# One block of a hybrid encoder in fp32: the gate/up products in another order, with banks of their own, their left factors made between the first products, and h stored by GpSimd

## The chip, the cores and the metric

The kernel runs on one core of a Trainium2 chip. The metric is the device time of one launch in microseconds; lower is better. The time before is 2817.62 us, the median of three runs (2817.23 to 2819.71).

## The reference

One layer of an encoder on a sequence of 512 tokens of width 2048, all in fp32: a mixing sub-layer (convolution, pooling, gated DeltaNet, Mamba-2), a cross-attention into 256 memory tokens, and a SwiGLU feed-forward with an inner width of 5632. Each sits between two norms and is added to the stream. What matters here is the third:

```python
def swiglu_ffn(h, w_gu, w_down):
    gate, up = jnp.split(h @ w_gu, 2, axis=-1)
    return (jax.nn.silu(gate) * up) @ w_down
...
x = x + rmsnorm(swiglu_ffn(rmsnorm(x, g[FFN_PRE]), ffn_w_gu[l], ffn_w_down[l]), g[FFN_POST])
```

## The kernel before

An fp32 product is made of three TensorE passes: each operand is split into a high part (a cast on ScalarE, L976) and a low part (source minus high part on VectorE, L977), and `mul3` (L168 to L171) adds high times high, high times low and low times high into one PSUM bank. The two large feed-forward products are worked by a seven-product scheme of 2x2 blocks in the manner of Strassen and Winograd: the activations give the left factors L1 to L7, the weights the right factors, and products M1 to M7 (numbered so in the code) are added into a few PSUM banks. On page and rows, L2h or B5l are left factors (number, high or low part) of the gate/up stage and of the down stage.

**Gate/up** (`gate_up`, L1019; `block`, L1073) runs over 44 blocks of 128 inner columns. A block loads four weight tiles of 0.5 MB (B11, B12, B21, B22), makes sums of them on VectorE (L1009 to L1016), splits each right factor into `whi` and `wlo`, and runs the products in `ORDER` (2, 1, 5, 6, 7, 3, 4), 24 matmuls each. M2 and M1 go into the two halves of one bank (`B` and `A` in `begin`, L1054); M2's half is copied out as `f_x` by ScalarE (L1067). M6, M7 and M4 are then added onto M1's half, where M6 is copied out as `f_y` (L1094) before M7 is added; M5 and M3 share a second bank `Cc`. The finished h tile (128 x 512) is stored to DRAM from SyncE's queue (L1108), which also loads all weights.

For the first five blocks M2 and M1 are made ahead of the others (`begin`), three of them while the second half of the normalised activations is still on its way. `left_parts` (L979) then makes L5, L6, L7, L3 and L4 for both 128-row halves (`sub`), all before block 0's five other products; their memory is opened at once, and the weight buffers `rp` and the work tiles `tp` are laid where the activations `stg` lay, so they wait for the last factor.

**Down** (`down`, L1124; `panel`, L1152) takes h back in five chunks of eight tiles, makes left factors B1 to B7 of each, and runs two panels per chunk, again seven products in `ORDER`, 24 matmuls of 512 columns each, with weights of 1 MB a tile (`rawB`, L1158). Results go to DRAM by GpSimd, which adds there.

Order on an engine is the order in which a list scheduler places the instructions; each engine's queue runs in that order, and SyncE's too: a store that waits holds up the loads behind it.

Of the kernel before, what the change touches and what calls it, by code (L numbers as in the profile page):

```python
# [7 lines left out]
F32 = mybir.dt.float32  # L8
# [7 lines left out]
P = 128  # L16
# [44 lines left out]

def build(tc, x, mem, norm_g, w_in, conv_a_w, pool_w, pool_scale, gdn_conv_w, gdn_A_log,
# [13 lines left out]
    es_act, es_ps, es_wp, es_stg, es_early = (ExitStack() for _ in range(5))  # L76
# [810 lines left out]
    def phase2(act):  # L887
        with ExitStack() as s0:
# [14 lines left out]
            stg = pool("stg", 8, "right", es_stg)  # L903
            yp = pool("yp2", stack=s0)
            pl2 = pool("adp2", stack=s0)
            xT = [[[stg.tile([P, 4, 256], F32, name="stg") for _ in range(2)] for _ in range(2)] for _ in range(2)]
# [66 lines left out]
    ORDER = (2, 1, 5, 6, 7, 3, 4)  # L973
# [5 lines left out]
    def left_parts(A11, A12, A21, A22, tmp, L, given=()):  # L979


        tt = nc.vector.tensor_tensor
        for m, a in ((2, A12), (1, A11)):
            if m not in given:
                split3(L[m], a)
                yield
        tt(tmp, A21, A22, op=ALU.subtract)
        split3(L[5], tmp)
        yield
        tt(tmp, tmp, A11, op=ALU.subtract)  # L990
        split3(L[6], tmp)
        yield
        tt(A21, A11, A21, op=ALU.subtract)
        split3(L[7], A21)
        yield
        tt(A12, A12, tmp, op=ALU.add)
        split3(L[3], A12)
        yield
        split3(L[4], A22)
        yield  # L1000

    def right_parts(B11, B12, B21, B22, new, begun=False):

        tt = nc.vector.tensor_tensor
        if not begun:
            yield B21
            yield B11
        p, t2 = new(), new()
        tt(p, B11, B12, op=ALU.add)  # L1009
        yield p  # L1010
        tt(t2, p, B22, op=ALU.add)
        yield t2
        tt(B12, B12, B22, op=ALU.add)
        yield B12
        yield B22
        tt(t2, t2, B21, op=ALU.add)  # L1016
        yield t2

    def gate_up(xT, L, begun):  # L1019

        with ExitStack() as s0:
            lp = pool("lp", 2, stack=s0, reuse_waits="tile")
            for m in ORDER[2:]:
                L[m] = [(lp.tile([P, 4, 256], F32R, name=f"L{m}h"), lp.tile([P, 4, 256], F32R, name=f"L{m}l"))
                        for _ in range(2)]
            with ExitStack() as s1:
# [4 lines left out]
                for _ in ORDER[2:]:  # L1031
                    for g in parts:
                        next(g)
# [293 lines left out]
```

## Time and profile before

| | us |
|---|---|
| median of three runs | 2817.62 |
| the profiled execution | 2815.95 |
| its span in the profile | 2814.2 |
| TensorE busy in the span | 2721.0 |
| VectorE, ScalarE, GpSimd busy | 1868.8, 1220.6, 115.9 |
| gate/up stage, first product of block 0 to last of block 43 | about 1411 to 2350 |
| down stage, both panels of five chunks | about 2363 to 2740 |

Times in rows are from the span's start; the execution is 1.75 us longer than its span. PE is TensorE, PEld its weight loads, DVE VectorE, ACT ScalarE, POOL GpSimd, SP SyncE. Matmuls overlap, so a busy PE says little about its pace: pace is read from start to start. `[x <-Y]` after a row is the idle time of the engine before it and what ended it.

### The profile page before, as it was taken

The page shows a single profiled execution, that of the slowest core. Times are in us where ns is not written, and L with a number is a line of the kernel's source. Part 1 is how long each engine was busy: PE and PEld are TensorE (multiplying, and loading weights), DVE is VectorE, ACT ScalarE, POOL GpSimd, SP SyncE. Part 2 cuts the span into 40 slices and gives each one's busy share as a digit, 9 for nine tenths or more (in the row PEclk, how much of TensorE's full clock was granted, in tenths as well). Part 3 has the DMA queues.
Part 4 walks back from the last instruction along what each step waited for, and adds up shares of the span by engine and source line. Part 5 has one row for each costly group of instructions (what it writes and reads, how often), then busy time and mean ns, then how long its engine had stood idle before and what let it go on. Part 6 is the DMA issues. An engine that isn't in the chain of part 4 may idle for free. (4 is left out here: it accounts for less than half of the span.)

```text
span 2814.2 us, 39887 instructions
## 1 busy us (share of the span) xinstructions
PE 2721.0 (97%) x15890; PEld 2384.8 (85%) x15890; DVE 1868.8 (66%) x2693; ACT 1220.6 (43%) x1874; POOL 115.9 (4%) x175
## 2 busy tenths in 40 slices
PE   8999999999999999999869999999999997999997
PEld 6788788878788878888769999999999997888885
DVE  5736557455752273343788777777777778999976
ACT  5623433233552253433554444444444444556542
POOL 0000001100000010000000000000000000000002
PEclk9999999999999999999989999999999999999998
DMA  8633322335574277523644333333333335577656
GB/s 294 226 102 95 89 68 79 113 120 168 191 276 176 96 260 240 165 90 131 212 157 148 117 117 113 124 109 117 113 114 123 112 110 213 186 192 198 169 144 222
DMA packets 161589, 428.38 MB, mean 152 GB/s; under 512 B 18157, under 2 KB 29306, under 8 KB 150522
## 3 DMA queue, kind: packets, MB, share of 16 engines
q1 hardware_dynamic: 146490, 367.10, 39.3%
q0 software_dynamic: 14912, 58.73, 7.6%
q8 instruction: 124, 2.03, 0.3%
q14 instruction: 63, 0.52, 0.1%
HBM read 351.30 MB, written 74.47 MB: 151 GB/s over the span
## 5 line engine op out<-in xcount | busy, mean ns | idle before, releaser
L154 DVE SCALAR_TENSOR_TENSOR wlo<-raw,PA,whi 128x512 fp32r<-128x512 f32 x368 | 263.2, 747 | 297.9 <-ACT whi L153 297.7
L153 ACT ACTIVATE whi<-raw,PA 128x512 fp32r<-128x512 f32 x368 | 247.7, 718 | 398.0 <-PE mm L170 213.8
L169 PE MATMUL mm<-act,whi 128*128 128x512 f32 x832 | 330.4, 397 | 0.0
L171 PE MATMUL mm<-act,wlo 128*128 128x512 f32 x832 | 327.3, 393 | 0.0
L170 PE MATMUL mm<-act,whi 128*128 128x512 f32 x832 | 326.8, 393 | 0.0
L976 ACT CAST whi<-raw 128x1024 fp32r<-128x1024 f32 x176 | 184.8, 1050 | 308.8 <-PE mm L170 262.2
L169 PE MATMUL mm<-whi,act 128*128 128x512 f32 x640 | 252.2, 395 | 1.9 <-ACT act L150 1.9
L170 PE MATMUL mm<-wlo,act 128*128 128x512 f32 x640 | 251.2, 393 | 1.8 <-DVE wlo L154 1.8
L171 PE MATMUL mm<-whi,act 128*128 128x512 f32 x640 | 250.5, 392 | 0.2 <-DVE act L151 0.2
L977 DVE TENSOR_TENSOR wlo<-raw,whi 128x1024 fp32r<-128x1024 f32 x176 | 215.5, 1226 | 49.2 <-ACT whi L976 48.7
L151 DVE TENSOR_TENSOR wlo<-raw,whi 128x1024 fp32r<-128x1024 f32 x92 | 112.4, 1224 | 192.9 <-ACT whi L150 192.8
L976 ACT CAST whi<-sum 128x1024 fp32r<-128x1024 f32 x132 | 138.5, 1050 | 215.8 <-PE mm L170 213.8
L977 DVE TENSOR_TENSOR wlo<-sum,whi 128x1024 fp32r<-128x1024 f32 x132 | 161.3, 1223 | 74.9 <-ACT whi L976 74.9
L171 PEld LDWEIGHTS mm<-act,wlo 128*128 128x128 f32 x832 | 156.8, 188 | 32.1 <-issue 0.5
L169 PEld LDWEIGHTS mm<-act,whi 128*128 128x128 f32 x832 | 156.9, 189 | 31.0 <-issue 0.7
L170 PEld LDWEIGHTS mm<-act,whi 128*128 128x128 f32 x832 | 156.8, 188 | 30.9 <-issue 0.7
L150 ACT CAST whi<-raw 128x1024 fp32r<-128x1024 f32 x92 | 96.8, 1053 | 186.7 <-PE mm L171 139.1
L169 PEld LDWEIGHTS mm<-whi,act 128*128 128x128 f32 x640 | 120.8, 189 | 28.3 <-ACT act L150 3.7
L170 PEld LDWEIGHTS mm<-wlo,act 128*128 128x128 f32 x640 | 120.9, 189 | 26.9 <-DVE wlo L154 2.7
L171 PEld LDWEIGHTS mm<-whi,act 128*128 128x128 f32 x640 | 120.6, 188 | 25.3 <-DVE act L151 0.6
L171 PE MATMUL mm<-L2h,wlo 128*128 128x256 f32 x352 | 101.1, 288 | 17.6 <-DVE wlo L977 17.6
L976 ACT CAST whB<-rawB 128x1024 fp32r<-128x1024 f32 x80 | 84.0, 1053 | 53.8 <-PE mm L171 52.1
(541 smaller groups left out, 7268.6 us busy)
## 6 DMA issues: line engine op xcount, KB each, us to landing
raw<-in_w_gu_dram SPq DMA_DIRECT2D x186, 512.0 KB, 3.4
raw<-in_w_in_dram SPq DMA_DIRECT2D x88, 512.0 KB, 3.6
rawB<-in_w_down_dram SPq DMA_DIRECT2D x40, 1024.0 KB, 6.2
raw<-in_xa_wkv_dram SPq DMA_DIRECT2D x64, 512.0 KB, 4.6
raw<-in_w_out_dram SPq DMA_DIRECT2D x32, 512.0 KB, 3.7
raw<-in_xa_wo_dram SPq DMA_DIRECT2D x32, 512.0 KB, 6.0
raw<-in_xa_wq_dram SPq DMA_DIRECT2D x32, 512.0 KB, 3.8
raw<-vw_d SPq DMA_DIRECT2D x28, 512.0 KB, 4.2
```

The costliest lines, as they stand in the source:

```text
L150: nc.scalar.copy(hi, src)
L151: nc.vector.tensor_tensor(lo, src, hi.bitcast(F32), op=ALU.subtract)
L153: nc.scalar.activation(hi, src, AF.Copy, scale=scale)
L154: nc.vector.scalar_tensor_tensor(lo, src, scale, hi.bitcast(F32), op0=ALU.mult, op1=ALU.subtract)
L169: nc.tensor.matmul(o, ah, bh, start=start, stop=False, skip_group_check=reopen)
L170: nc.tensor.matmul(o, ah, bl, start=False, stop=False, skip_group_check=reopen)
L171: nc.tensor.matmul(o, al, bh, start=False, stop=stop, skip_group_check=reopen)
L976: nc.scalar.copy(hl[0], src)
L977: nc.vector.tensor_tensor(hl[1], src, hl[0].bitcast(F32), op=ALU.subtract)
```

## The change

The order of the products becomes 1, 2, 6, 5, 7, 3, 4 in both stages, with weight tiles loaded in the order in which this needs them. In gate/up, M1 has the half bank `A` for itself and M2 a bank of the `ps` pool; what is copied out as `f_x` is M1, and the gate is formed from M2's bank. Block 0 runs in the order 5, 6, 7, 4, 3, and one left factor is made ahead of each of its products, with the early products of blocks 3 and 4 in between; memory of the activations is given back in three steps. The tile for h is single, and GpSimd's queue stores it.

```diff
-    ORDER = (2, 1, 5, 6, 7, 3, 4)
+    ORDER = (1, 2, 6, 5, 7, 3, 4)
+    FIRST = (5, 6, 7, 4, 3)
...
+        def sums(m):
+            if m in have:
+                return
+            have.add(m)
+            if m == 5:
+                tt(tmp, A21, A22, op=ALU.subtract)
+            elif m == 6:
+                sums(5)
+                sums(7)
+                tt(A11, tmp, A11, op=ALU.subtract)
+            elif m == 7:
+                sums(5)
+                tt(A21, A11, A21, op=ALU.subtract)
+            elif m == 3:
+                sums(6)
+                tt(A12, A12, A11, op=ALU.add)
+        for m in order:
+            sums(m)
+            split3(L[m], {1: A11, 2: A12, 3: A12, 4: A22, 5: tmp, 6: A11, 7: A21}[m])
+            if m == 7:
+                sums(3)
+            yield m
...
+            rp = pool("rp", 3, stack=s0, reuse_waits="tile")
+            tp = pool("tp", 2, stack=s0, reuse_waits="tile")
+            first = block(0, L, rp, tp, begun[0], FIRST)
+
+            def step():
+                for g in parts:
+                    next(g)
+                next(first)
+            step()
+            step()
+            begun[3] = begin(3, L, tp)
+            step()
             es_stg.close()
+            factor("lp4", 4)
+            step()
+            begun[4] = begin(4, L, tp)
+            es_a22.close()
+            factor("lp3", 3)
+            step()
...
+        if begun:
+            A, g = begun
+        else:
+            A, B = half(mm, "mm"), half(ps, "ps")
+            X, g = tl("x"), tl("g", 3)
+            product(A, split_w(next(parts)), L, 1)
+            nc.scalar.copy(X, A)
+            product(B, split_w(next(parts)), L, 2)
+            gate(g, B, X)
+        Cc = half(ps, "ps")
...
-        h = tp.tile([P, T], F32, name="f_h")
+        h = tp.tile([P, T], F32, name="f_h", bufs=1)
...
-        nc.sync.dma_start(h_d[j], h)
+            if m != order[-1]:
+                yield
+        nc.gpsimd.dma_start(h_d[j], h)
...
-            if m == 2:
+            if m == 1:
                 X = new("eX")
-                copy(X, B)
-            elif m == 1:
+                copy(X, A)
+            elif m == 2:
                 for t in range(2):
-                    tt(X[:, t], A[t], X[:, t], op=ALU.add)
+                    tt(X[:, t], B[t], X[:, t], op=ALU.add)
```

The changed line numbers are larger by 8 to 49 (`mul3` is at L176 to L179, the split at L988 and L989).

**First place.** TensorE in a block of gate/up before: the first matmul of each run of one left factor, and those that wait (`ps` is the bank `Cc`).

```order
L169 MATMUL mm<-L2h,whi 128x256 [waits Activation_49]
L171 MATMUL mm<-L2h,wlo 128x256 [waits DVE_49]
...
L169 MATMUL ps<-L5h,whi 128x256 [waits Activation_49]
L171 MATMUL ps<-L5h,wlo 128x256 [waits DVE_49]
...
L169 MATMUL mm<-L1h,whi 128x256 [waits Activation_49]
...
L169 MATMUL mm<-L6h,whi 128x256 [waits DVE_49]
...
L169 MATMUL mm<-L7h,whi 128x256 [waits Activation_49]
```

And now:

```order
L177 MATMUL mm<-L1h,whi 128x256 [waits Activation_49]
L179 MATMUL mm<-L1h,wlo 128x256 [waits DVE_49]
...
L177 MATMUL ps<-L2h,whi 128x256 [waits Activation_49]
...
L177 MATMUL mm<-L6h,whi 128x256 [waits Activation_49]
...
L177 MATMUL ps<-L5h,whi 128x256
L179 MATMUL ps<-L5h,wlo 128x256 [waits DVE_49]
...
L177 MATMUL mm<-L7h,whi 128x256 [waits Activation_49]
```

Before, 11 matmuls of M5 stand between M2 and M1 and the other 13 behind M1, and M3 is cut in the same way around M7. Now each product stands whole, with one product of 24 matmuls between a product and the next one that is added to its bank.

**Second place.** VectorE where the left factors are made, before (`tmp` and `stg` are sums and activations, `wlo<-raw` a right factor's low part).

```order
L977 TENSOR_TENSOR L5l<-tmp_11498,L5h 128x1024 [waits Activation_49]
...
L977 TENSOR_TENSOR L7l<-stg,L7h 128x1024 [waits Activation_49]
L977 TENSOR_TENSOR L3l<-stg,L3h 128x1024 [waits Activation_49] x2
L977 TENSOR_TENSOR L4l<-stg,L4h 128x1024 x2
L977 TENSOR_TENSOR wlo<-raw,whi 128x1024 [waits DMAHW4_49]
L977 TENSOR_TENSOR wlo<-raw,whi 128x1024 [waits DMAHW5_49]
```

And now:

```order
L989 TENSOR_TENSOR L5l<-tmp,L5h 128x1024 [waits Activation_49]
L1027 TENSOR_TENSOR sum<-raw 128x1024 [waits DMAHW6_49,DMAHW4_49,DMASW2_49]
...
L1009 TENSOR_TENSOR stg<-stg 128x1024
L1105 TENSOR_TENSOR f_g<-mm,f_x 128x256 [waits PE_49]
L989 TENSOR_TENSOR wlo<-sum,whi 128x1024 [waits Activation_49]
...
L1030 TENSOR_TENSOR sum<-sum,raw 128x1024 [waits DMAHW7_49]
L989 TENSOR_TENSOR L6l<-stg,L6h 128x1024 [waits Activation_49]
```

The first right factor's low part stood behind all ten left factors' low parts; now M5's stands behind two of them, and M6's after three.

**Third place.** SyncE at the end of gate/up, before and now (`hq` is a quarter of a chunk of h).

```order
L1120 DMA hq<-h_d 128x4x256 [waits DMAHW6_49]
L1108 DMA h_d<-f_h 128x512 [waits DMAHW7_49,DVE_49]
L1158 DMA rawB<-in_w_down_dram 128x2048 [waits DMAHW0_49,PE_49]
L1158 DMA rawB<-in_w_down_dram 128x2048 [waits DMAHW1_49,PE_49]
L1158 DMA rawB<-in_w_down_dram 128x2048 [waits DMAHW2_49]
```

```order
L1168 DMA hq<-h_d 128x4x256 [waits DMAHW3_49]
L1208 DMA rawB<-in_w_down_dram 128x2048 [waits DMAHW4_49,PE_49]
L1208 DMA rawB<-in_w_down_dram 128x2048 [waits DMAHW5_49,PE_49]
L1208 DMA rawB<-in_w_down_dram 128x2048 [waits DMAHW6_49,PE_49]
L1208 DMA rawB<-in_w_down_dram 128x2048 [waits DMAHW7_49]
```

And ScalarE there, before and now:

```order
L976 CAST B7h<-hq 128x1024 [waits DVE_49,Activation_49]
L976 CAST B6h<-tmp 128x1024 [waits DVE_49]
L976 CAST B3h<-hq 128x1024 [waits DVE_49]
L976 CAST whB<-rawB 128x1024 [waits DMAHW2_49,DMASW3_49,DMASW1_49]
L976 CAST whB<-rawB 128x1024 [waits Activation_49]
```

```order
L988 CAST B7h<-hq 128x1024 [waits DVE_49,Activation_49]
L988 CAST whB<-rawB 128x1024 [waits DMAHW4_49]
L988 CAST whB<-rawB 128x1024 [waits DMASW4_49,DMASW5_49,DMASW3_49,DMASW6_49,DMASW2_49,DMASW7_49,DMASW1_49,DMASW0_49]
L988 CAST B6h<-hq 128x1024 [waits DVE_49]
L988 CAST whB<-rawB 128x1024 [waits DMAHW5_49]
```

The store of the last h no longer stands ahead of the down weights' loads; two casts of the first right factor stand ahead of B6 and B3, and the second of them waits for all of GpSimd's stores.

## Rows read from the trace of the kernel before

**Rows 1.** The page's busy times by engine: us busy, share of the span, instructions.

```profile
PE 2721.0 (97%) x15890; PEld 2384.8 (85%) x15890; DVE 1868.8 (66%) x2693; ACT 1220.6 (43%) x1874; POOL 115.9 (4%) x175
```

**Rows 2.** Stretches of the span: length, then busy us and instructions of each engine, granted TensorE clock (1.00 is 2.4 GHz, 0.50 is 1.2 GHz), DMA share, GB/s.

```profile
1426.00:1450.00 24.00, 12.00 (x97) 11.11 (x95) 23.07 (x39) 14.23 (x17) 0.00 (x0) 0.93 0.20 66
1450.00:1470.00 20.00, 11.02 (x70) 10.82 (x70) 16.22 (x17) 5.97 (x8) 0.00 (x0) 0.66 0.62 205
1470.00:1500.00 30.00, 29.78 (x244) 29.40 (x245) 24.91 (x27) 12.24 (x18) 0.00 (x0) 1.00 0.48 153
1600.00:1700.00 100.00, 100.00 (x818) 98.24 (x817) 76.12 (x87) 42.37 (x59) 0.00 (x0) 1.00 0.35 114
2340.00:2380.00 40.00, 25.74 (x141) 22.05 (x140) 33.65 (x32) 18.94 (x21) 0.00 (x0) 0.83 0.74 278
2420.00:2520.00 100.00, 100.00 (x443) 82.81 (x442) 93.60 (x81) 61.14 (x70) 7.66 (x10) 1.00 0.70 201
```

**Rows 3.** What TensorE's weight loads waited for from 1488 to 2350: us in total, times, the longest.

```profile
PEld mm L169 <- ACT f_y L1094: 8.1, 43, 0.5
PEld mm L169 <- ACT f_x L1067: 6.9, 39, 0.2
```

**Rows 4.** TensorE, ScalarE and VectorE in one block of gate/up, in order of time on each: start, length, engine, line, operation.

```profile
2312.60 0.28 PE L170 MATMUL ps<-L5l,whi 128*128 128x256 f32 x1
2312.85 0.38 PE L169 MATMUL mm<-L1h,whi 128*128 128x256 f32 x1
2313.07 0.28 PE L170 MATMUL mm<-L1l,whi 128*128 128x256 f32 x1
...
2311.48 1.06 ACT L976 CAST whi<-sum 128x1024 fp32r<-128x1024 f32 x1 [1.55 <-PE mm L170]
2312.43 0.37 ACT L1067 COPY f_x<-mm 128x256 f32<-128x256 f32 x1
...
2311.27 0.42 DVE L1107 SCALAR_TENSOR_TENSOR f_h<-f_t,f_z 128x256 f32<-128x256 f32 x1
...
2331.87 0.42 DVE L1107 SCALAR_TENSOR_TENSOR f_h<-f_t,f_z 128x256 f32<-128x256 f32 x1
```

**Rows 5.** VectorE at the start of gate/up, in order of time.

```profile
1435.30 0.41 DVE L1068 TENSOR_TENSOR f_g<-mm,f_x 128x256 f32<-128x256 f32 x1
1435.63 1.21 DVE L987 TENSOR_TENSOR tmp<-stg 128x1024 f32<-128x1024 f32 x1
...
1454.85 2.35 DVE L977 TENSOR_TENSOR L4l<-stg,L4h 128x1024 fp32r<-128x1024 f32 x2
1457.12 3.48 DVE L977 TENSOR_TENSOR wlo<-raw,whi 128x1024 fp32r<-128x1024 f32 x3
1464.35 1.23 DVE L977 TENSOR_TENSOR wlo<-raw,whi 128x1024 fp32r<-128x1024 f32 x1 [3.75 <-ACT whi L976]
```

**Rows 6.** TensorE in the same place and shortly before it: the waits, two matmuls at the lower clock, and the first matmul of block 1.

```profile
1402.57 0.79 PE L170 MATMUL mm<-wlo,pth 128*128 128x512 f32 x1 [3.92 <-DVE wlo L151]
...
1438.25 0.39 PE L169 MATMUL mm<-L1h,whi 128*128 128x256 f32 x1 [3.63 <-ACT f_x L1067]
1458.39 0.58 PE L171 MATMUL mm<-L2h,wlo 128*128 128x256 f32 x1 [15.16 <-DVE wlo L977]
...
1460.05 0.41 PE L169 MATMUL mm<-L2h,whi 128*128 128x256 f32 x1
1460.26 0.41 PE L170 MATMUL mm<-L2l,whi 128*128 128x256 f32 x1
...
1487.57 0.28 PE L169 MATMUL ps<-L5h,whi 128*128 128x256 f32 x1
```

**Rows 7.** From gate/up to down: the last matmul of gate/up and the first of down, then ScalarE, VectorE and SyncE's queue there.

```profile
2349.94 0.28 PE L171 MATMUL mm<-L4h,wlo 128*128 128x256 f32 x1
2363.62 1.22 PE L169 MATMUL mm<-whB,B2h 128*128 128x512 f32 x2 [13.40 <-ACT whB L976]
2365.40 0.80 PE L170 MATMUL mm<-wlB,B2h 128*128 128x512 f32 x1 [0.56 <-DVE wlB L977]
...
2388.17 0.39 PE L169 MATMUL mm<-whB,B7h 128*128 128x512 f32 x1
...
2355.04 1.04 ACT L976 CAST B7h<-hq 128x1024 fp32r<-128x1024 f32 x1 [1.28 <-DVE hq L993]
...
2362.52 3.89 ACT L976 CAST whB<-rawB 128x1024 fp32r<-128x1024 f32 x4 [1.70 <-DMA rawB<-in_w_down_dram]
...
2360.79 2.28 DVE L1009 TENSOR_TENSOR sumB<-rawB 128x2048 f32<-128x2048 f32 x1
...
2351.58 0.33 SPq L1108 DMA_DIRECT2D h_d<-f_h  x1
2352.01 1.87 SPq L1158 DMA_DIRECT2D rawB<-in_w_down_dram  x4
```

**Rows 8.** Stores of a tile: SyncE's of h, GpSimd's of a tile of the same size, and how long GpSimd's stores of L883 and L1174 (512 KB, added in DRAM) took from issue to landing.

```profile
h_d<-f_h SPq DMA_DIRECT2D x44, 256.0 KB, 2.0
vw_d<-at_e POOLq DMA_DIRECT2D x32, 256.0 KB, 5.6
...
DMA to landing us min/median/max: 3.2/5.6/8.2
...
DMA to landing us min/median/max: 5.2/5.3/10.4
```

More of the change, by code (lines that the diff above doesn't have):

```diff
@@ L75, in build @@
     sm = pool("smp", 4)
[L76 removed]
+    es_act, es_ps, es_wp, es_a12, es_a22, es_stg, es_early = (ExitStack() for _ in range(7))
     pool("padl").tile([P, 32], F32, name="pad")
@@ L1019, in gate_up @@
     def gate_up(xT, L, begun):
         with ExitStack() as s0:
[L1022 to L1026, printed above, removed]
-                tmp = pool("tmpp", 1, stack=s1, reuse_waits="tile")
-                parts = [left_parts(xT[0][0][sub], xT[1][0][sub], xT[0][1][sub], xT[1][1][sub],
-                                    tmp.tile([P, 4, 256], F32, name=f"tmp{sub}"),
-                                    {m: L[m][sub] for m in ORDER}, (1, 2)) for sub in range(2)]
-                for _ in ORDER[2:]:
-                    for g in parts:
-                        next(g)
@@ L1034, in gate_up, with factor @@
-            es_stg.close()
-            rp = pool("rp", 3, stack=s0, reuse_waits="tile")
-            tp = pool("tp", 2, "right", s0, reuse_waits="tile")
-            for j in range(3, 5):
-                begun[j] = begin(j, L, tp)
-            for j in range(HT):
-                block(j, L, rp, tp, begun.get(j))
+            def factor(name, *ms):
+                lp = pool(name, 2, stack=s0, reuse_waits="tile")
+                for m in ms:
+                    L[m] = [(lp.tile([P, 4, 256], F32R, name=f"L{m}h"), lp.tile([P, 4, 256], F32R, name=f"L{m}l"))
+                            for _ in range(2)]
@@ new lines, in gate_up @@
+            factor("lp", 6, 5, 7)
+            tmp = pool("tmpp", 2, stack=s0, reuse_waits="tile")
+            parts = [left_parts(xT[0][0][sub], xT[1][0][sub], xT[0][1][sub], xT[1][1][sub],
+                                tmp.tile([P, 4, 256], F32, name="tmp"),
+                                Lazy(lambda m, sub=sub: L[m][sub]), FIRST) for sub in range(2)]
+            rp = pool("rp", 3, stack=s0, reuse_waits="tile")
+            tp = pool("tp", 2, stack=s0, reuse_waits="tile")
+            first = block(0, L, rp, tp, begun[0], FIRST)
@@ L1136, in down @@
                 lb.tile([P, 4, 512], F32, name="rawB", bufs=6)
+            for i in "hl":
+                for _ in range(5):
+                    lb.tile([P, 2, 512], F32R, name=f"w{i}B", bufs=5)
             for _ in range(2):
```

121 lines of the change are left out of this document (58 added, 63 removed).

## The prediction

> **What bounds the kernel now.** I read the busy times first: TensorE is busy for 2721.0 us, 97% of the span, no other engine for more than 66% [rows 1]. So a gain must come from stretches in which TensorE idles or runs below its pace. The table by stretches shows two that the change touches: 1426 to 1470, where TensorE is busy for 23 of 44 us and the granted clock falls to 0.66, and 2340 to 2380, busy 25.7 of 40 us [rows 2]. Between them a stretch such as 1600 to 1700 is 100% busy, with VectorE at 76% [rows 2]; there only the pace can tell. The waits of the weight loads name two small ones that come once a block: 39 on `f_x` and 43 on `f_y` [rows 3]. In time order the break is seen: matmuls of 256 columns follow each other by 0.12 us, but M1's first comes 0.25 us after M5's tenth, and the next 0.22 us later [rows 4], 0.47 for two steps of 0.12, or 0.23 lost. ScalarE's copy of `f_x`, behind a cast, ends at 2312.80, and M1 starts at 2312.85 [rows 4]. From one h to the next are 20.60 us (2311.27 to 2331.87) [rows 4]; 168 matmuls at 0.12 are 20.16, so a block loses 0.44 us, which is the two breaks.
>
> **Steady blocks.** The change takes away the reason for both breaks. M1 has its own bank, and what is added onto it next is M6, a whole product (24 x 0.12 = 2.88 us) later. At M1's end ScalarE has a cast (1.06) and the copy (0.37) to do, done about 1.4 us after it: 1.5 us of slack. M7 waits for the copy of M6's bank and has M5 between instead of 11 matmuls of M3 (1.3 us, which fell short by 0.2): again 1.4 against 2.88. The right factors of three products fit in their buffers, so the cast for the third product ahead starts at a product's end and both parts are there about 2.5 us later (1.06 + 1.22), 3 us before they are needed. VectorE has the same instructions as before. I count 39 blocks with both breaks and 5 with M7's alone: 39 x 0.44 + 5 x 0.22 = 18.3 us. Bounds: nothing (the breaks come back elsewhere) to 19.
>
> The store of h goes from SyncE's queue to GpSimd's. No engine waits for the landing until the single h tile is written again: behind M3 of the next block, about 17.3 us after M4's last matmul, while h is complete some 3 us after it, so 14.5 us are free. A GpSimd store of the same 256 KB lands in 5.6 us, at most 8.2 [rows 8]. I cost it at nothing in the blocks; the cover is gone at 14.5 us.
> The Trainium skill has a rule against this move ("SBUF — State Buffer", section "SBUF: two separate sides"): GpSimd writes the descriptors of its own DMAs, and VectorE in a two-port mode locks it out, so that the DMA appears blocked. The trace speaks against it here: with VectorE busy for 93.6% [rows 2] GpSimd's adding stores of twice the size land in 5.3 us, at most 10.4 [rows 8]; by the rule the last rival below would be likelier, by the rows it isn't.
>
> **The start of gate/up.** VectorE sets the pace: from 1435.30 to 1460.6 it has no gap [rows 5], and it makes all ten left factors before the first right factor (1457.12). TensorE waits for that one 15.16 us [rows 6], and runs at 1.2 GHz for a while after (0.21 a matmul) [rows 6]. At 1487.57 block 1 begins [rows 6].
> Now the factors are made between the products. I follow VectorE with its own durations: an operation of 128x1024 takes 1.13 us back to back (two from 1454.85 to 1457.12), a small one 0.33 (1435.30 to 1435.63) [rows 5]. In its new order six large and three small stand before M5's low part: 1435.3 + 6.8 + 1.0 = 1443.1, done at 1444.3. A small one and five large later M6's starts at 1450.3, done at 1451.5. Then come two right factors of block 3's early products, the rest of L6, L7, two sums, L4: with M6's own, eleven large and two small, so M7's starts at 1463.4, done 1464.6; four large and a small one later M4's starts at 1468.5, done 1469.7. TensorE meanwhile does M5 (to 1447.2), M6 and block 3's early products (to 1460.2), M7 (to 1467.5); from 1469.7 it lacks nothing, and what it owes before block 1 is M4 and 70 matmuls, 94 x 0.12 = 11.3: block 1 begins at 1481.0, 6.6 us sooner. Two things can take from it. Idle of 3.9 us was followed by matmuls of 0.79 and more at 1402.57 [rows 6], and M7 stands behind 4.4 us of idle; a 24-matmul product costs 2.2 more at 0.21, of which VectorE's pace hides about half. And a weight tile of block 4 can load only after M7's split. I take 5 us; bounds 0 and 7. VectorE has no more to do than before, so there is no debt later: the first factors of block 1 are done 1 to 3 us ahead of their products by the same counting.
>
> **From gate/up to down.** TensorE ends gate/up at 2350.06 (call it E) and waits until 2363.62, in earnest until 2365.40; four products of the first panel are done at 2388.17, E + 38.1 [rows 7]. The loads of the down weights stood behind the last h store, which SyncE issues at 2351.58; they go at 2352.01 and the first cast waits for them until 2362.52 [rows 7]. Now they stand behind no store and wait only for factors that TensorE is done with 6 to 11 us before E. But ScalarE and VectorE keep B4, B5 and B7 ahead of the right factors, in turn with each other: B7's cast starts at 2355.04 before, E + 5.0 [rows 7], and the first right factor's follows at E + 6; the second waits for the last h store, E + 1.6 + 5.6 = E + 7.2, which is when its turn comes. Behind B5, a sum and B7, VectorE makes the first low part at about E + 8.3 to 9.5, and M1 runs from there, 5.8 us sooner than M2 before. Then M6 asks for two sums where M5 asked for one: after three more low parts and B6's (to E + 13.9) VectorE has two sums of 2.28 [rows 7], a left sum 1.1, a small one 0.6 and another 2.28, so M6's low part is ready at E + 23.5, when M2 has ended at about E + 22. M6 and M5 are 48 x 0.226 (100 us for 443 [rows 2]) = 10.8: four products are done at E + 34.3, 3.8 sooner. A late store costs up to 3 (10.4 for 7.2); I take 3 us, bounds -2 and +6.
>
> **Later panels.** 168 matmuls each, TensorE at 100%, VectorE at 93.6% [rows 2] with the same work in another order. I take 0; if M6's second sum comes late in each, 9 x 2.28 = 20 us are lost, the bound.
>
> **Sum.** 18.3 + 5 + 3 = 26.3 us off the profiled execution's 2815.95: 2789.7. The median of the runs is 1.67 above that execution, so 2791.3; forecast 2791, with the likeliest case's own range 2786 to 2797.
>
> **Rivals.** All start from 2817.6.
> - The start gives nothing, because the gaps between products leave the clock at 1.2 GHz. At 0.213 a matmul M6 and block 3's products last until 1466.4, M7 until 1471.5, M4's factor follows at 1473.1 and M4 ends at 1478; with 70 matmuls at 0.12 to 0.213 block 1 begins between 1486.6 and 1493 instead of 1487.57. For it: at 1402 slow matmuls follow an idle of 3.9 us [rows 6]. Against: the stretch to 1450, busy half its time, kept 0.93 [rows 2]. Price: gain 0 there, time 2796.
> The Trainium skill ("TensorE: Matmul & The Clock Gate", section "HAM oscillation — how this bites in real kernels") tells of products that wait between them and each start slow; by that rule it would be this rival.
> - The breaks in the blocks stay, because ScalarE's copies come later than I read. It would need 1.5 us more delay; its queue has one cast ahead of each. Then 3 + 5 remain: 2810.
> - The two sums for M6 delay each later panel by one: 26.3 - 20 = 6: 2811. For it: 93.6% of VectorE. Against: the weights come well ahead, and TensorE waited for nothing there before.
> - Slower: GpSimd's stores land late. With a landing beyond 14.5 us VectorE stops at each of 43 blocks; at 16 us that is 43 x 1.5 = 64, less 26: 2856. From 15.1 us on it is slower than before (26.3 / 43 = 0.6). Nothing here took over 10.4.
>
> **Chances.** Forecast 0.62, start without gain 0.15, breaks stay 0.09, sums in each panel 0.07, late stores 0.03, better than the likeliest range 0.04. The range 2783 to 2806 holds the first two, the last, and what lies between them; the others are left out. About 0.2% (5.6 us) is what a measurement of this kernel can tell from no change: 2812. The two at 2810 and 2811 fall on either side of it, half each; faster 0.62 + 0.15 + 0.04 + 0.08 = 0.89, same 0.08, slower 0.03.
>
> **What would show it.** From h to h 20.16 us in the steady blocks, and no rows of weight loads waiting for `f_x` or `f_y`; if 20.6, the second rival. Block 1's first product at 1481 to 1483; the clock between 1440 and 1475 tells the first rival. M1's first matmul at E + 7 to 10, four products done near E + 35. GpSimd's landings of h between 3 and 8 us. TensorE 100% busy in the panels. The forecast is wrong if TensorE's idle moves into waits for right factors in the blocks.

## The result, and the profile after

The changed kernel takes 2794.60 us (median of four runs, 2792.55 to 2795.19), the kernel before 2818.66 beside it (2817.23 to 2819.95): a ratio of 0.9913, 95% interval 0.9896 to 0.9931, 24 us. The forecast was 2791, from 2783 to 2806. The profiled execution took 2794.72, its span is 2792.9, 21.3 less than before.

A single number hides that the blocks and the passage came out and that the start and the closing stage did not. I cut both spans at the same events: gate/up's first matmul, block 1's first, gate/up's last, the first matmul of the first panel's B7 (four products are done then), the last panel's last matmul, the last matmul of all.

| us | before | after | gain | forecast |
|---|---|---|---|---|
| up to gate/up's first matmul | 1411.91 | 1412.36 | -0.45 | 0 |
| start, to block 1 | 75.66 | 74.20 | 1.46 | 5 |
| blocks 1 to 43 | 862.37 | 843.71 | 18.66 | 18.3 |
| passage, to four products done | 38.23 | 34.22 | 4.01 | 3 |
| the rest of the panels | 358.82 | 358.82 | 0 | 0 |
| closing stage | 52.94 | 55.71 | -2.77 | 0 |
| from there to the end | 14.2 | 13.9 | 0.3 | 0 |

The first line is nearly the same code in both; over all profiles of this study it lies between 1408 and 1415, so one span can be off by some 3 us through it alone.

**Busy times and stretches**, which answer to [rows 1] and [rows 2], of the changed kernel:

```profile
PE 2711.8 (97%) x15890; PEld 2385.9 (85%) x15890; DVE 1861.8 (67%) x2693; ACT 1222.6 (44%) x1874; POOL 139.5 (5%) x219
```

```profile
1426.00:1450.00 24.00, 17.91 (x121) 16.89 (x119) 21.46 (x40) 10.27 (x15) 0.00 (x0) 0.86 0.44 166
1450.00:1470.00 20.00, 13.20 (x81) 12.19 (x82) 18.30 (x19) 10.37 (x15) 0.00 (x0) 0.85 0.17 60
1470.00:1500.00 30.00, 29.43 (x226) 28.75 (x226) 24.70 (x29) 12.35 (x16) 0.55 (x1) 0.93 0.54 180
1600.00:1700.00 100.00, 100.00 (x835) 100.00 (x835) 77.69 (x89) 43.49 (x61) 2.69 (x5) 1.00 0.36 119
2320.00:2360.00 40.00, 31.35 (x165) 26.46 (x165) 34.63 (x32) 20.53 (x26) 1.08 (x2) 0.87 0.65 249
2400.00:2500.00 100.00, 100.00 (x443) 82.84 (x442) 93.51 (x80) 60.32 (x69) 8.51 (x11) 1.00 0.68 201
```

The fourth line is the steady part: 835 matmuls in 100 us where 818 stood, and the weight loads busy without a gap. "100% busy" said the same before; the count tells the difference. In the first three lines TensorE does more of its work early, but the clock is below 1.00 in all three, where before it was so in the first two.

**One block**, which answers to [rows 4]: TensorE, ScalarE, VectorE.

```profile
2292.83 0.28 PE L179 MATMUL mm<-L1h,wlo 128*128 128x256 f32 x1
2292.95 0.28 PE L177 MATMUL ps<-L2h,whi 128*128 128x256 f32 x1
...
2295.83 0.28 PE L177 MATMUL mm<-L6h,whi 128*128 128x256 f32 x1
...
2293.03 1.05 ACT L988 CAST whi<-sum 128x1024 fp32r<-128x1024 f32 x1 [1.50 <-PE mm L178]
2293.99 0.36 ACT L1125 COPY f_x<-mm 128x256 f32<-128x256 f32 x1
...
2293.89 0.42 DVE L1152 SCALAR_TENSOR_TENSOR f_h<-f_t,f_z 128x256 f32<-128x256 f32 x1
...
2314.05 0.42 DVE L1152 SCALAR_TENSOR_TENSOR f_h<-f_t,f_z 128x256 f32<-128x256 f32 x1
```

M2 starts 0.12 behind M1's last matmul. The copy of `f_x` ends at 2294.35 and M6, which needs it, starts at 2295.83: 1.5 us of slack, as worked out. From h to h are 20.16 us. From 1488 to 2330 neither TensorE nor its weight loads have a wait that the trace lists.

**The start**, which answers to [rows 5] and [rows 6]: VectorE, then TensorE.

```profile
1431.03 1.42 DVE L965 TENSOR_SCALAR ad_x<-ad_x,nr_r 128x1024 f32<-128x1024 f32 x2 [2.06 <-DMA x_d<-ad_x]
...
1437.15 0.41 DVE L1105 TENSOR_TENSOR f_g<-mm,f_x 128x256 f32<-128x256 f32 x1
...
1445.10 1.22 DVE L989 TENSOR_TENSOR wlo<-sum,whi 128x1024 fp32r<-128x1024 f32 x1
...
1464.25 0.42 DVE L1105 TENSOR_TENSOR f_g<-mm,f_x 128x256 f32<-128x256 f32 x1 [1.70 <-PE mm L179]
...
1467.19 1.22 DVE L989 TENSOR_TENSOR wlo<-raw,whi 128x1024 fp32r<-128x1024 f32 x1
...
1473.56 0.42 DVE L1142 TENSOR_TENSOR f_z<-f_z,mm 128x256 f32<-128x256 f32 x1 [1.75 <-PE mm L179]
1473.90 1.22 DVE L989 TENSOR_TENSOR wlo<-sum,whi 128x1024 fp32r<-128x1024 f32 x1
```

```profile
1466.11 0.39 PE L177 MATMUL mm<-L7h,whi 128*128 128x256 f32 x1 [1.97 <-ACT whi L988]
...
1468.46 0.58 PE L179 MATMUL mm<-L7h,wlo 128*128 128x256 f32 x1 [1.85 <-DVE wlo L989]
1468.84 0.41 PE L177 MATMUL mm<-L7h,whi 128*128 128x256 f32 x1
1469.06 0.41 PE L178 MATMUL mm<-L7l,whi 128*128 128x256 f32 x1
...
1473.11 0.41 PE L179 MATMUL mm<-L7h,wlo 128*128 128x256 f32 x1
...
1486.56 0.28 PE L177 MATMUL mm<-L6h,whi 128*128 128x256 f32 x1
```

Behind two waits M7 runs at 0.21 a matmul, 1.2 GHz, and ends at 1473.3; I had it end at 1467.5. VectorE itself waits for TensorE here (1.70 before `f_g`, 1.75 before `f_z`), which it did nowhere in [rows 5]. From gate/up's first matmul to block 1's, 83 matmuls of 256 columns follow the one before by 0.20 to 0.225 us without a wait, where 37 did before the change.

**From gate/up to down**, which answers to [rows 7]:

```profile
2330.27 0.28 PE L179 MATMUL mm<-L4h,wlo 128*128 128x256 f32 x1
2337.42 1.22 PE L177 MATMUL mm<-whB,B1h 128*128 128x512 f32 x2 [6.87 <-ACT whB L988]
...
2354.39 0.50 PE L178 MATMUL mm<-wlB,B6h 128*128 128x512 f32 x1 [0.54 <-DVE wlB L989]
...
2364.49 0.39 PE L177 MATMUL mm<-whB,B7h 128*128 128x512 f32 x1
...
2338.61 2.35 DVE L989 TENSOR_TENSOR wlB<-rawB,whB 128x1024 fp32r<-128x1024 f32 x2
```

M1 starts 7.15 us behind gate/up's last matmul, four products are done 34.22 behind it; 7 to 10 and 34.3 were worked out.

**The closing stage**, of which the prediction has no row: SyncE's queue before, then now.

```profile
2737.56 0.33 SPq L1246 DMA_DIRECT2D gB<-in_norm_g_dram  x1
2737.98 0.38 SPq L1250 DMA_DIRECT2D ad_x<-x_d  x1
2752.15 2.53 SPq L1241 DMA_DIRECT2D raw<-in_w_last_dram  x2
```

```profile
2722.37 0.33 SPq L1296 DMA_DIRECT2D gB<-in_norm_g_dram  x1
2722.75 0.42 SPq L1300 DMA_DIRECT2D ad_x<-x_d  x1
2728.47 2.53 SPq L1291 DMA_DIRECT2D raw<-in_w_last_dram  x2
```

The last panel's last matmul starts at 2746.99 and at 2723.31. So gB and the rows of x (1 MB each) were issued 9.4 us ahead of it and are now issued 0.9 ahead, just before the last weight tiles. ScalarE waited 5.70 us for the first of these tiles before and 7.42 now.

**GpSimd's stores of h**, which answer to [rows 8]:

```profile
DMA to landing us min/median/max: 2.3/3.9/5.9
```

### The profile page after: what moved, and what is told of

It is laid out like the page before. It is cut to its first block, busy times and chain, and to the rows that moved or that the text cites. A ratio compares the mean times of both kernels' runs of the same rounds, so it can differ in the third digit from the quotient of the medians.

```text
span 2792.9 us, 39958 instructions
## 1 busy us (share of the span) xinstructions
PE 2711.8 (97%) x15890; PEld 2385.9 (85%) x15890; DVE 1861.8 (67%) x2693; ACT 1222.6 (44%) x1874; POOL 139.5 (5%) x219
## 3 DMA queue, kind: packets, MB, share of 16 engines
q1 hardware_dynamic: 140154, 355.57, 38.2%
## 5 line engine op out<-in xcount | busy, mean ns | idle before, releaser
L179 PE MATMUL mm<-act,wlo 128*128 128x512 f32 x832 | 326.6, 393 | 0.0
L988 ACT CAST whi<-raw 128x1024 fp32r<-128x1024 f32 x176 | 184.6, 1049 | 272.0 <-PE ps L178 133.3
L989 DVE TENSOR_TENSOR wlo<-sum,whi 128x1024 fp32r<-128x1024 f32 x132 | 161.4, 1222 | 134.9 <-ACT whi L988 134.7
L179 PE MATMUL mm<-whi,act 128*128 128x512 f32 x640 | 251.0, 393 | 0.2 <-DVE rsq_t L151 0.2
L988 ACT CAST whi<-sum 128x1024 fp32r<-128x1024 f32 x132 | 138.3, 1049 | 214.0 <-PE mm L178 129.6
L989 DVE TENSOR_TENSOR wlo<-raw,whi 128x1024 fp32r<-128x1024 f32 x176 | 215.4, 1225 | 19.8 <-ACT whi L988 14.3
L179 PEld LDWEIGHTS mm<-act,wlo 128*128 128x128 f32 x832 | 156.3, 188 | 32.2 <-issue 0.5
L179 PEld LDWEIGHTS mm<-whi,act 128*128 128x128 f32 x640 | 120.9, 189 | 25.2 <-DVE act L159 0.6
L988 ACT CAST whB<-rawB 128x1024 fp32r<-128x1024 f32 x80 | 84.1, 1053 | 51.3 <-PE mm L179 50.8
L177 PE MATMUL mm<-L1h,whi 128*128 128x256 f32 x352 | 101.3, 288 | 4.4 <-ACT f_x L1099 4.4
```

The costliest lines, as they stand in the source:

```text
L177: nc.tensor.matmul(o, ah, bh, start=start, stop=False, skip_group_check=reopen)
L179: nc.tensor.matmul(o, al, bh, start=False, stop=stop, skip_group_check=reopen)
L988: nc.scalar.copy(hl[0], src)
L989: nc.vector.tensor_tensor(hl[1], src, hl[0].bitcast(F32), op=ALU.subtract)
```

## The experiments

All numbers of a row come from one kernel's runs and its one profile; ratios are to the kernel before on the same chip. The four stages are those of the table above.

| run | median | ratio, 95% interval | start | blocks | passage | closing |
|---|---|---|---|---|---|---|
| before | 2818.66 | 1 | 75.7 | 862.4 | 38.2 | 52.9 |
| changed | 2794.60 | 0.9913 (0.9896 to 0.9931) | 74.2 | 843.7 | 34.2 | 55.7 |
| e_again | 2796.28 | 0.9920 (0.9908 to 0.9933) | 74.0 | 843.7 | 34.8 | 56.8 |
| e_order | 2807.31 | 0.9957 (0.9943 to 0.9971) | 74.7 | 854.0 | 34.1 | 56.0 |
| e_bank | 2892.14 | 1.0257 (1.0243 to 1.0271) | 74.2 | 941.1 | 33.7 | 55.8 |
| e_store | 2796.20 | 0.9917 (0.9904 to 0.9931) | 74.8 | 843.7 | 34.9 | 55.8 |
| e_ahead | 2796.96 | 0.9915 (0.9900 to 0.9930) | 74.0 | 843.7 | 34.4 | 55.8 |
| e_fill | 2792.67 | 0.9901 (0.9887 to 0.9916) | 70.4 | 843.7 | 33.7 | 58.0 |
| e_aheadfill | 2796.42 | 0.9923 (0.9909 to 0.9938) | 74.3 | 843.7 | 34.4 | 56.0 |
| e_scale | 2794.86 | 0.9919 (0.9904 to 0.9934) | 74.0 | 843.7 | 34.8 | 56.6 |
| e_down5 | 2794.82 | 0.9909 (0.9894 to 0.9923) | 74.2 | 843.7 | 34.4 | 56.8 |
| e_exit | 2793.27 | 0.9910 (0.9894 to 0.9927) | 74.2 | 843.7 | 32.1 | 58.1 |
| e_noreserve | 2792.21 | 0.9900 (0.9883 to 0.9916) | 74.5 | 843.7 | 34.2 | 52.2 |
| e_all | 2784.78 | 0.9875 (0.9857 to 0.9894) | 71.6 | 843.7 | 33.3 | 53.6 |

The intervals reach 3 to 5 us to each side. A difference of 2 or 3 us between two rows is read from the stage columns, which agree between profiles to 0.8 in the start, to 1.2 in the passage, to 0.1 in the blocks, and to 2.4 in the closing stage (55.7 to 58.1 wherever the change's three reservation lines stand).

**The changed kernel again** (e_again, no edit).

> The changed kernel as it is, a second time, to see which of its differences come back. 2794.6 us as measured first, within 2. Theory: blocks 1 to 43 (from block 1's first product to gate/up's last matmul) take 843.7 us again, four products of the first panel are done 34.2 us after that last matmul, panels 2 to 10 take 342.5; these are set by the order of the work. What is set by chance (when idle meets the clock, when a load lands) need not come back: the closing stage took 55.7 us from the last panel's end in the first profile and 52.95 before; if the 2.8 us are the change's, they are there again, if not, it is near 53 here. In the same way block 1 began 74.2 us after the first gate/up product, 75.65 before: by the clock theory this varies by 1 to 3 us between profiles, by the theory that VectorE alone sets it, it does not.

2796.28 us. Blocks and panels came back to 0.01. The closing stage's loss came back too, larger by 1.0 (56.75), so it belongs to the change. My guess that the start varies by 1 to 3 us between profiles was wrong; the eight profiles with this start lie within 74.0 to 74.8.

**The old order in the blocks, with the new banks** (e_order).

```diff
-                for _ in block(j, L, rp, tp, begun.get(j), ORDER[2:]):
+                for _ in block(j, L, rp, tp, begun.get(j), (5, 6, 7, 3, 4)):
```

> The steady blocks run 5, 6, 7, 3, 4 behind M1 and M2, as before the change, with the new banks kept. Theory (my prediction's): the break before M7 came from the order, since M7 stands right behind the product whose copy it waits for, with 11 matmuls of M3 between; it comes back in 43 blocks with 0.22 each: 9.5 us more than the changed kernel, 2804, from h to h 20.38, weight loads wait for f_y 43 times and for f_x never. Rival: M1's own bank removed both breaks: no difference, 2794.6.

Blocks 1 to 43 take 10.3 us more, 0.24 for each. The weight loads' waits from 1490 to 2336 have one row, and none for `f_x`:

```profile
PEld mm L177 <- ACT f_y L1139: 7.8, 43, 0.2
```

So the order removes the break before M7, 10.3 of the blocks' 18.7 us. The other break stays away with the old order behind M1 and M2: the banks of their own, with M1 ahead of M2, remove it.

**M2 back in M1's bank, with the new order** (e_bank).

```diff
-            A, B = half(mm, "mm"), half(ps, "ps")
+            both = mm.tile([P, 512], F32, name="mm")
+            A, B = both[:, 0:256], both[:, 256:512]
```

With M2's start between M1 and M6 in one bank, the sums that begin with M1 are changed; the instructions and their sizes are not.

> M2 is put back into M1's bank, as its second half; the order of the products stays new. Theory: M2 waits until ScalarE has copied M1's half out, with only two matmuls of M5 between them; the copy takes 0.4 us and a cast of 1.06 may stand ahead of it, so it is done 0.4 to 1.4 us behind M1, less 0.24 for the two: 0.2 to 1.2 us in each of 39 blocks, 8 to 47 us, 2803 to 2841, and weight loads wait for f_x 39 times. Rival: the order alone removed the breaks: 2794.6.

The blocks take 97.3 us more, 2.5 for each of 39, twice the upper bound. Both theories missed the scheduler: it no longer finds M2 ready behind M1, puts two matmuls of M5 in between, and leaves only seven between M6 and M7. TensorE's waits from 1490 to 2420:

```profile
PE ps L177 <- ACT whi L988: 39.7, 39, 1.0
PE mm L177 <- ACT f_y L1140: 17.2, 38, 0.5
PE mm L177 <- DVE f_g L1105: 7.2, 18, 1.8
```

M5's pair waits 1.0 us for its own cast, the old break before M7 is back with 0.5, and M6 must wait until `f_g` is read from the other half. The rows count idle between modelled ends; from start to start a block with all three takes 22.66 us (M1 at 2001.57, the next at 2024.23), 2.50 more than 20.16. It isn't a clean test of the copy alone, but shows that the new order stands only with a bank of its own for M1. The Trainium skill ("PSUM — Partial Sum Buffer", section "PSUM: the matmul accumulator") gives a reason beside time: the start of a second group in a bank makes the first group's next matmul overwrite its sum instead of adding. No row of a trace shows that; the output of this run, off by 0.41 in relative terms, agrees with it. Before the change M2 was complete when M1 began, so the old order could share a bank.

**h stored from SyncE's queue again** (e_store).

```diff
-        nc.gpsimd.dma_start(h_d[j], h)
+        nc.sync.dma_start(h_d[j], h)
```

> h is stored from SyncE's queue again. Theory: nothing in the blocks (from h to h 20.16 either way); at the passage to the down stage the weight loads stand behind the last h store again, and the first product of the first panel starts some 13 to 15 us after gate/up's last matmul instead of 7, four products are done up to 6 us later: 2797 to 2801. Rival 1: the loads wait for TensorE and not for the store, and nothing changes: 2794.6. Rival 2: GpSimd's stores cost time in the blocks that no row names: some us faster.

Blocks 843.7, as forecast. At the passage the loads do stand behind the store again, and ScalarE's first cast waits 2.25 us for them:

```profile
2335.07 0.33 SPq L1155 DMA_DIRECT2D h_d<-f_h  x1
2335.50 2.03 SPq L1208 DMA_DIRECT2D rawB<-in_w_down_dram  x4
...
2341.78 1.99 ACT L988 CAST whB<-rawB 128x1024 fp32r<-128x1024 f32 x2 [2.25 <-DMA rawB<-in_w_down_dram]
```

M1 starts 9.4 us behind gate/up's last matmul instead of 7.15, and four products are done at 34.9, against 34.2 and 34.8 in the changed kernel's two profiles; up to 6 us more was expected. So the queue of the store gives nothing in the blocks, and at the passage nothing that stands out from the spread of the profiles: it isn't what made the 4 us. SyncE's stores land in 4.1 us here in the median, GpSimd's of the same tile in 3.9.

**All left factors ahead of the products** (e_ahead). The calls that make the five left factors stand in front of `begin(3)`, `begin(4)` and the products of block 0, with memory given back in the same steps:

```diff
-                next(first)
...
+            begun[3] = begin(3, L, tp)
+            begun[4] = begin(4, L, tp)
```

> All left factors are made ahead of block 0's five products and of blocks 3 and 4's early products, as before the change; all else is new. Theory by what was measured: block 1 begins some 75.6 us after the first gate/up product instead of 74.1, 1.5 us more in all: 2797. By my prediction's working the interleaving is worth 5 to 6.6, and block 1 would begin at 79 to 81, 2800. Rival: the order of block 0's products (5, 6, 7, 4, 3) gave the 1.5, not the interleaving: 74.1.

73.95: the interleaving brings nothing here. That is the rival's number; its reason, the order of block 0's products, no run tried. TensorE waits for the first right factor in one piece, and starts block 1 at the same time:

```profile
1458.34 0.58 PE L179 MATMUL mm<-L2h,wlo 128*128 128x256 f32 x1 [9.55 <-DVE wlo L989]
```

**Idle matmuls in TensorE's gaps at the start** (e_fill). 20 stand ahead of block 2's M1, 16 in M5, 24 between M6 and M7; their bank is not read.

```diff
+            def fill(n, m, s=0, i=0):
+                o = ps.tile([P, 512], F32, name="ps")[:, 0:256]
+                a = L[m][s][i]
+                for i in range(n):
+                    nc.tensor.matmul(o, a[:, i % 4, 0:P], a[:, i % 4], start=i == 0, stop=i == n - 1)
...
+            fill(20, 1)
...
+            step(16, 5, 1, 1)
...
+            step(24, 7, 1, 1)
```

> 60 matmuls without use (their bank is not read) stand in TensorE's gaps at the start of gate/up: 20 ahead of block 2's M1, 16 in M5, 24 between M6 and M7; nothing else is changed, though the scheduler turns a few of VectorE's operations round. Theory: the start gave 1.5 us instead of 5 because idle before M6 and M7 left TensorE at 1.2 GHz, M7 took 0.22 a matmul and all that VectorE does behind it was late; with the gaps filled the granted clock stays at 1.00 there, M7 takes 2.9 us instead of 4.7 to 5.3, and block 1 begins 71 us after the first gate/up product instead of 74.1: 2792. Rival: VectorE's pace alone sets it; the clock is full and block 1 begins within 1 us of 74.1. Third: the fillers themselves delay products, up to 2 us more.

Block 1 begins at 70.4, 3.8 us sooner; with the same filling in e_all below, 2.5 sooner. M7 runs at 0.12, three matmuls from one of these rows to the next:

```profile
1466.45 0.28 PE L177 MATMUL mm<-L7h,whi 128*128 128x256 f32 x1
...
1466.81 0.28 PE L177 MATMUL mm<-L7h,whi 128*128 128x256 f32 x1
```

```profile
1426.00:1450.00 24.00, 19.49 (x154) 18.32 (x153) 21.68 (x36) 10.98 (x14) 0.00 (x0) 0.99 0.40 155
1450.00:1470.00 20.00, 18.33 (x125) 17.48 (x126) 19.17 (x20) 11.10 (x14) 0.00 (x0) 0.83 0.31 105
1470.00:1500.00 30.00, 29.72 (x247) 29.52 (x247) 28.58 (x33) 12.83 (x18) 0.84 (x2) 1.00 0.56 184
```

The clock is not full from 1450 to 1470 (M6, behind an idle of 3.55, pays there), so my 1.00 was too much; but it is 1.00 from 1470 on, where the changed kernel had 0.93. VectorE's waits for TensorE before `f_g` and `f_z` are 0.83 and nothing, instead of 1.70 and 1.75.

**Idle matmuls with all factors ahead** (e_aheadfill; 90 of them, 70 in the long wait).

```diff
+            fill(20, 1)
...
+            fill(70, 5)
```

> As the run with all left factors ahead (block 1 began 73.95 us after the first gate/up product), with 90 matmuls without use in TensorE's gaps ahead of block 3's early products, 70 of them where it waits 10 us for the first right factor. It tells what making the factors between the products is worth when the clock is held in both: interleaved and filled, block 1 began at 70.4. Theory: the 32 matmuls of M2 behind the wait take 0.12 instead of 0.195, block 1 begins 2.3 us sooner, at 71.6, and the interleaving is worth about 1 us more, no more, because VectorE has the same work in either order. Rival (my prediction's working): the interleaving is worth 5 or more at the same clock, and block 1 begins at 75 or later. Third: the clock falls all the same, 73.95.

74.3, nothing won: TensorE still waits 4.04 us for the factor after the 70 have run out, and the granted clock from 1450 to 1470 is 0.83, as in the run before. Between the two filled runs, making the factors between the products is worth 3.9 us (74.3 to 70.4); 5 to 6.6 was forecast, and "about 1" in this run's theory. It isn't a clean price, since the clock is not the same throughout: from 1426 to 1450 it is 0.89 here and 0.99 in e_fill. Without the filling nothing of it is left (e_ahead).

**No wait for the store of the rows** (e_scale). The scaled rows go to a free tile instead of in place.

```diff
-            nc.vector.tensor_scalar(xs[1][:, qs], xs[1][:, qs], n[:, 1:2], None, op0=ALU.mult)
+            nc.vector.tensor_scalar(y[:, tiles[1], qs], xs[1][:, qs], n[:, 1:2], None, op0=ALU.mult)
...
```

> The normalised rows are written into the free tile y instead of in place, so that ScalarE and VectorE don't wait for the store of the rows by GpSimd; all else is the changed kernel. Theory: in the changed kernel block 0's four weight tiles are loaded from 1418 on beside that store, whose landing VectorE waits for 2.0 to 2.5 us in each of eight profiles (0.41 before the change); without the wait VectorE's first operation of the gate comes some 2 us sooner, and block 1 begins at 72 us after the first gate/up product instead of 74.1: 2793. Rival: the low clock behind it takes the 2 us back, as it took the rest of the gain, 74: 2795.

The wait is gone, and the start is 74.0 as without the edit. VectorE scales 2.0 us sooner behind gate/up's first matmul (16.7 instead of 18.7), but then waits 2.66 us for TensorE's transposes:

```profile
1425.83 1.42 DVE L965 TENSOR_SCALAR y<-ad_x,nr_r 128x1024 f32<-128x1024 f32 x2
1429.91 4.88 DVE L973 TENSOR_TENSOR stg<-ps,PA 128x512 f32<-128x512 f32 x8 [2.66 <-PE ps L971]
```

The first operation of the gate behind them comes at 25.5, not sooner than in the eight profiles with this start (24.8 to 25.5). TensorE runs matmuls ahead of the transposes in its queue without a wait from 1421.84 on, 27 of them at 0.21 up to 1427.8, 2.5 us more than at 0.12. So in this profile the low clock took the 2 us back, as the rival says, but ahead of the gate's operation and not behind it. One profile doesn't settle what the wait is worth: the transposes start 20.1 us behind gate/up's first matmul here, and after 17.9 in four of those eight. The edit moves one thing more: two of block 0's four weight loads, which stood beside the store from 1418 on, are issued only from 1433.88 on, and the second store of the rows lands in 5.5 us as before the change, instead of 7.1.

**M5 before M6 in the down stage alone** (e_down5), **and with 56 idle matmuls ahead of it** (e_exit).

```diff
+    DOWN = (1, 2, 5, 6, 7, 3, 4)
...
-            if i + 2 < len(ORDER):
-                ws[ORDER[i + 2]] = factor()
+            if i + 2 < len(DOWN):
+                ws[DOWN[i + 2]] = factor()
```

In e_exit besides:

```diff
+        if c == 0 and n == 0:
...
+            for i in range(56):
+                nc.tensor.matmul(o[:, 0:256], a[:, i % 4, 0:P], a[:, i % 4], start=i == 0, stop=i == 55)
```

> In the down stage alone M5 comes before M6 (1, 2, 5, 6, 7, 3, 4); gate/up as changed. Theory: behind M2 TensorE waits for M6's low part, which needs two sums of 2.28 us where M5 needs one; with M5 first four products are done 0.9 us sooner, 33.3 us behind gate/up's last matmul instead of 34.2 and 34.8, and panels stay 342.5: 2794. Rival 1 (the sums weigh more, VectorE has no gap there): 2.3 us sooner, 31.9. Rival 2: no difference at all, since M7's factor sets the end of the four.

> Between gate/up's last matmul and the first panel 56 matmuls without use stand in TensorE's gap of 7 us, and the down stage runs 1, 2, 5, 6, 7, 3, 4 as in the run before that made no difference (34.4). Theory: there the granted clock was 0.50 for 10.2 us behind the gap, and M1's first half ran at 0.43 a matmul instead of 0.23; VectorE is just ahead with M5 first. With the gap filled the clock stays at 1.00 and four products are done 2 us sooner, 32.4 behind gate/up's last matmul: 2793. Rival: VectorE's row of sums and low parts sets it, the clock is full and it stays at 34.

The order alone changes nothing (34.4). With the gap filled the clock from 2330 to 2345 is 1.00 instead of 0.67, and four products are done at 32.1. The filling with M6 first wasn't tried. The stretch with the order alone, then with both:

```profile
2330.00:2345.00 15.00, 7.02 (x16) 5.04 (x17) 14.64 (x14) 8.63 (x10) 0.54 (x1) 0.67 0.64 245
```

```profile
2330.00:2345.00 15.00, 13.11 (x80) 11.36 (x80) 14.97 (x14) 8.54 (x10) 0.54 (x1) 1.00 0.59 226
```

**The reservation lines taken out** (e_noreserve). The diff of the change adds three lines to `down` that set aside memory for `whB` and `wlB` ahead of the sums.

```diff
-            for i in "hl":
-                for _ in range(5):
-                    lb.tile([P, 2, 512], F32R, name=f"w{i}B", bufs=5)
```

> Taken out of the changed kernel: the three lines that reserve memory for the down stage's split right factors ahead of the sums. Theory: by these lines the tile for the last norm's weights (gB) came to lie where TensorE reads until the last panel ends, so that its load and one of 1 MB behind it are issued 0.9 us before the last panel's end instead of 9.4, and collide with the last two weight tiles of the closing stage; without the lines gB is loaded early again, and the closing stage (from the last panel's last matmul to its own) takes 53 us as before the change instead of 55.7 and 56.7: some 3 us less than the changed kernel, 2792. Rival: the late landing has another cause, and the stage takes 55.7 again. The passage from gate/up to down is not expected to change by more than 0.5 us.

Closing stage 52.2 instead of 55.7. The last panel's last matmul starts at 2722.26 here; gB is issued 9.5 us ahead of it again, and ScalarE waits 5.57 for the weight tile instead of 7.42.

```profile
2712.79 0.33 SPq L1293 DMA_DIRECT2D gB<-in_norm_g_dram  x1
```

In SyncE's queue gB's load waits 12.1 us for TensorE's matmuls with the three lines, and 7.6 us for VectorE's low part `wlB` without them, as before the change. That the tile came to lie elsewhere is read from these waits; the memory itself is in no row.

**All that helped** (e_all), and 24 idle matmuls ahead of the closing stage.

> All that helped, together, on the changed kernel: the 60 idle matmuls at the start of gate/up, the down stage with M5 first and 56 idle matmuls ahead of it, the reservation lines taken out, and one new thing: 24 idle matmuls between the last panel and the closing stage. Theory: the pieces stand at different places and add up: block 1 begins 70.4 us after the first gate/up product (74.1 in the changed kernel), four products are done 32.1 behind gate/up's last matmul (34.2 to 34.8), the closing stage takes 52.2 (55.7 to 56.8): 3.7 + 2.3 + 3.5 = 9.5 off 2795.4 (the middle of 2794.6 and 2796.3), 2786. The new one holds the clock for the closing stage's first products, where it was 0.50 for 6.8 us: up to 2.5 us more, 50. Rival 1: the closing stage is set by its weights' loads and splits, and stays 52.2. Rival 2: what is won at one place is lost at the next, where TensorE then waits: 2791 or more.

2784.78 us, 9.8 and 11.5 under the changed kernel's two medians. In the profile the pieces don't add up in full: start 71.6 and passage 33.3 (the clock still falls for a while in both), closing 53.6, so the new idle matmuls there brought nothing. The three stages make 6.3 us of the difference to the changed kernel's profiles (74.1, 34.5 and 56.2 in the mean), where 9.5 were expected. Most of the rest, 3.6 us, lies ahead of gate/up, where nothing was changed and profiles differ by as much, so that 2784.78 lies near the expected 2786 partly by luck.

## Why the prediction was right, and where not

- **Steady blocks**, 18.3: right, 18.66, by the mechanism given: the order removes one break (10.3 us, e_order), the banks the other, and the new order needs M1's bank besides (e_bank). VectorE at 78% has no wait on its way. One of the five blocks counted with M7's break alone is block 0, which falls into the start, so the working gives 18.0 for blocks 1 to 43; and the matmul ahead of the break was M5's eleventh, not its tenth.
- **h by GpSimd**, nothing: right, both in the blocks and against SyncE at the passage. Landings of 2.3 to 5.9 us, 3.9 in the median, reach below the 3 to 8 expected and stay far from 14.5. The rule of the Trainium skill that I weighed ("SBUF — State Buffer", section "SBUF: two separate sides"), a GpSimd DMA that appears blocked by VectorE, shows at no landing here. No row tells whether VectorE runs in the mode that the rule names, so these runs don't put it to the test.
- **The start**, 5 (bounds 0 and 7): wrong, 1.46. The step that failed is "two things can take from it", where I let VectorE's pace hide half of the clock's cost and took off 1.6 in all. TensorE waits ahead of M5, M6 and M7; M5 runs at 0.12, but part of M6 and all of M7 at 0.21, and VectorE then waits for TensorE, 1.70 and 1.75 us. So little of the cost was hidden: counted from VectorE's first `f_g` (1437.15), M7's low part starts after 30.0 us where 28.1 was worked out, and M4's after 36.8 where 33.2 was. That `f_g` itself comes 24.8 us behind gate/up's first matmul and 23.4 before the change; the working doesn't have these 1.4, which come behind VectorE's wait for the store of the rows. The two, 3.6 and 1.4, are nearly all of the 5.1 between 6.6 and 1.46. The run with the gaps filled (e_fill) shows that the clock is the cause of most of it.
  It is the rival that I gave 0.15: it had block 1 begin at 1486.6 at the earliest, and it began at 1486.56. The closeness is partly luck, since gate/up began 0.45 us later than before and the gain is 1.46 and not 0. My reason against it (a stretch busy half its time kept 0.93) was one row from before the change. The rule of the Trainium skill named there ("TensorE: Matmul & The Clock Gate", section "HAM oscillation — how this bites in real kernels") agrees with the trace in part: M7, behind waits of 1.97 and 1.85 us, runs slow, M5, behind 1.41, does not. With the gaps filled the working was close: 75.7 to 70.4 is 5.3.
  What gives the 1.46 that is left isn't settled. It doesn't need the interleaving (e_ahead has it too). In e_ahead the first right factor's low part comes 17.4 us behind VectorE's first `f_g`, in the kernel before 21.8 [rows 5], because four low parts now stand behind it; I read it as that, and didn't try it.
- **The passage**, 3 (3.8 worked out): right in size (4.0), and the steps came out: behind the end of gate/up's last matmul (2330.39) the first low part starts after 8.2 us (8.3 worked out), M6's low part is used after 24.0 (23.5), four products are done after 34.1 (34.3). What failed is a reason: "they stand behind no store" isn't worth the gain. In e_store the loads are issued 1.95 us behind that end, as before the change, and yet ScalarE's first cast starts after 8.2 us and not after 12.5 [rows 7]; in both it waits for a load until then. What the working leaves out is the order of the loads: before, M2 came first and its tile, B21, was the third of four in the queue, now M1's, B11, is the first. I read the gain as that. The two casts of the first right factor also moved ahead of B6 and B3, and no run takes the two apart, but before the change the load alone kept the cast from starting sooner than 12.5. And "M6 asks for two sums where M5 asked for one" costs nothing that shows while the clock is low (e_down5).
- **Later panels**, 0: right, 358.82 both times.
- **A term that I left out**: 2.77 lost in the closing stage. The three reservation lines were in the diff, and I read them as bookkeeping. With them gB's load waits for TensorE until the last panel ends, and without them the loss is gone (e_noreserve). Of the 2.77, 1.72 are ScalarE's longer wait for the weight tile; besides, the granted clock over the stage is 0.91 where it was 0.94.

In the profiled pair the misses add up to 5 us: 3.5 and 2.8 too little against 0.4 and 1.0 too much, 21.3 gained of 26.3. The medians' 24 lies nearer the forecast because the profiled execution before was 2.7 us under the median of the runs that stand beside the changed ones, and the changed one at its own. So the forecast's nearness is partly luck: 2794.6 lies nearer to the first rival's 2796 than to 2791.

## What to carry to other kernels

When products are spread between the steps that feed them, count what the gaps do to the clock before counting the overlap: idle in many pieces can cost as much as one long wait, and matmuls without use in the gaps gave back 2.5 to 3.8 us at one place and 1.1 to 2.3 at another, in two profiles each. Give a partial sum that others are added onto a bank of its own, and put one whole product between it and the next. Look at which of several loads is needed first: at the passage that explains more than the queue of the store before them. Lines that only reserve memory belong in the sum: with three of them a load was issued 0.9 us ahead of a stage's end instead of 9.5.

## What the runs showed that was not expected

- Filling a gap helped where TensorE was late behind it, and not where VectorE was: the same kind of filling brought 3.8 us with factors between the products and nothing with all of them ahead.
- Sharing a bank between two products costs more through the scheduler's answer than through the copy that was feared: 2.5 us a block instead of 0.2 to 1.2.
- An early load can lengthen another engine's wait: with block 0's weights loaded beside it, VectorE waits 2.06 us for the store of the rows where it waited 0.41 before. Its second store lands in 7.1 us; before the change, and in e_scale, where two of these four loads come later, in 5.5. Taking that wait away gained nothing in the one profile of it, since VectorE then waited for transposes that stood behind slow matmuls in TensorE's queue.
